# Other places for the block sums' steps around two norms, and the second layer's add copies in the pool of temporaries

## The chip, the cores and the metric

The kernel runs on one core of a Trainium2 chip. The metric is the device time of one execution in microseconds (us), less being better. The core has a matrix engine (TensorE, PE in the profile), a vector engine (VectorE, DVE), a scalar engine (ScalarE, ACT), GpSimd (POOL) and an engine that mostly issues loads (SyncE, SP). Each works off its own list of instructions in order and waits at semaphores for the others.

## The reference, cut to what matters

A two-layer encoder trunk on 512 tokens of width 1024. Each layer is a mixer (mLSTM and memory attention in layer 0; band attention and memory attention in layer 1), and then a gated feed-forward part with a causal convolution of width 3 over the tokens. The change touches the feed-forward part of both layers.

```python
D_MODEL, SEQ, DEPTH, D_FF, FFN_CONV = 1024, 512, 2, 2816, 3

def rmsnorm(x, g):
    y = x * lax.rsqrt(jnp.mean(x * x, axis=-1, keepdims=True) + 1e-6)
    return y * g

def conv_ffn(h, w_up, conv_w, conv_b, w_down):
    u, g = jnp.split(h @ w_up, 2, axis=-1)     # 1024 -> 2 x 2816
    g = causal_dwconv(g, conv_w, conv_b)       # 3 taps over the tokens
    return (jax.nn.silu(g) * u) @ w_down       # 2816 -> 1024
...
x = x + conv_ffn(rmsnorm(x, g_ffn), w_up, conv_w, conv_b, w_down)   # in each layer
...
return rmsnorm(x, final_g)
```

## The kernel before, in words

Activations are held with features on the 128 partitions and the 512 tokens along the free axis. Each fp32 number is split into a high and a low part of a shorter type, and a product is three matmuls (`mm3`: high by high at L197, high by low at L198, low by high at L199). The split is a cast on ScalarE (L143) and a subtract on VectorE (L144). Tiles of weights are loaded raw ("wr"), and split into "wh" and "wl". In the order's listings the number behind such a name counts the tiles, and what stands behind `<-` is read.

The feed-forward part has 22 tiles of 128 hidden features (`ChannelMixer`). The first three are "plain": `plain(j)` makes the gate and the up product with `project()`, 24 matmuls of 128x512 each, the gate in a bank of tag "mm" and the up in one of tag "sc". The other 19 go through `step()` in a fixed order (`manual_schedule`, which keeps the written order of PE, ACT and DVE). A step multiplies blocks as Strassen's method does: seven block products of 12 matmuls 128x256, the first into the bank `r1` with the weight block `a11`. They need sums of blocks of the activations, which `block_sums()` makes ahead of the first step, as a generator (`forms`) of four steps. Each step scales two tiles on ScalarE (L788), does four subtracts on VectorE (L797), and splits four halves (four L143, four L144).

Where these four steps stand is set in two places. `EARLY` says, for each layer, how many are taken while the mixer's output projection is finished, behind which of its eight tiles. The rest are woven into the plain tiles: `weave(job, filler, each)` takes one step of the filler each time `each` has added up to 1 over the yields of the job, and whatever is left runs behind the third tile. `plain(0)` also weaves in `norm.finish()`: a cast and a subtract of the sum of squares, two matmuls with a matrix of ones (L302), and a few ScalarE and VectorE instructions (from L304) that leave the row by which all hidden tiles are scaled. Outside of `manual_schedule` the order on each engine is set by a scheduler that places instructions by its own estimates, so what stands where is read from the listings below.

Down products belong to the steps too. `down_products` makes a partial sum of one of the eight output tiles in a PSUM bank "tr"; `add` copies the bank on ScalarE into an SBUF tile (L823), from which GpSimd issues a DMA that adds it to the residual in DRAM, `xspill` (L824). The first two steps of a layer have four such adds, later ones two, 40 in a layer. The tiles come from the tag "bias", which has four buffers. In layer 1 two of these hold the last norm's gains from before the feed-forward part to the end. In a step the bank `r1` is used five times in turn; L892 is ScalarE's copy that empties it after the first, and L883 that after later ones. Tiles of tag "t" are temporaries of 128x512, eight buffers: a step keeps `up`, `u3`, `pre` and an accumulator in them.

## Time and profile before

| | us |
|---|---|
| Median of 3 runs | 1186.98 |
| Lowest and highest run | 1186.8, 1188.5 |
| The profiled execution | 1186.16 |
| Its span in the profile | 1184.4 |
| TensorE busy in it | 1166.5 |
| Mean granted clock of TensorE | 0.998 |

The span runs from the first to the last instruction that the profile records. In the rows of a timeline stand the start, the duration, the engine, the line and the operation, the tiles written and read, the shape and, in brackets, how long the engine had stood idle before it and which instruction ended that. A matmul's row is longer than the distance to the next, since matmuls overlap. In the table of windows "PEclk" is the clock that TensorE was granted, as a share of full speed.

### The profile page before, as it was taken

How to read it: one execution, taken by the hardware profiler on the slowest of the kernel's cores; microseconds unless marked ns; L12 is line 12 of the kernel's file. 1: busy time of each engine (PE TensorE's matmuls, PEld its weight loads, DVE VectorE, ACT ScalarE, POOL GpSimd, SP SyncE). 2: the span in 40 equal slices, each digit the busy share in tenths (PEclk: the TensorE clock that was granted, in tenths of full speed). 3: DMA queues.
4: the chain of work that ended last, by engine and by line, in shares of the span. 5: the costliest groups of instructions: out<-in, count | busy, mean ns of one | idle time of the engine just before them, and what ended most of it. 6: DMA issues, size and time to landing. Idle time of an engine off the chain costs nothing.

```text
span 1184.4 us, 19103 instructions
## 1 busy us (share of the span) xinstructions
PE 1166.5 (98%) x7149; PEld 1037.1 (88%) x7149; DVE 984.5 (83%) x1768; ACT 744.1 (63%) x1345; POOL 143.3 (12%) x238
## 2 busy tenths in 40 slices
PE   9999999999999999999999999999989999999997
PEld 9988888887899999999888888778789999999986
DVE  6776788788999988888788888997888998888865
ACT  6448677656666655555666666775756665555545
POOL 1111101010032211111020000101011111111100
PEclk9999999999999999999999999999999999999999
DMA  8645325344478766655662323236345766666551
GB/s 290 216 110 147 77 54 151 85 144 118 109 176 198 187 166 166 143 142 117 177 209 86 89 72 107 79 118 188 115 109 108 174 145 143 143 142 143 125 160 72
DMA packets 200623, 162.87 MB, mean 138 GB/s; under 512 B 8680, under 2 KB 176334, under 8 KB 200530
## 3 DMA queue, kind: packets, MB, share of 16 engines
q1 hardware_dynamic: 182066, 119.74, 34.5%
q0 software_dynamic: 17888, 40.86, 18.0%
q8 instruction: 56, 0.92, 0.3%
q10 hardware_dynamic: 576, 1.05, 0.2%
q14 instruction: 37, 0.30, 0.1%
HBM read 128.89 MB, written 36.66 MB: 140 GB/s over the span
## 4 chain that ended last, share of the span: by engine, by line
PE 82%; issue 12%; DVE 2%; ACT 1%; POOL 1%; DMA 1%; POOLq 0%; ACTq 0%; DVEq 0%
PE pmm L197 16%; PE pmm L198 16%; PE pmm L199 16%; PE ptr L198 6%; PE ptr L197 5%; PE ptr L199 5%; PE psc L198 4%; PE psc L197 4%; PE psc L199 4%; PE psc L603 2%; PE ptr L1414 1%; DVE wl L144 1%; DMA xspill<-bias 1%; PE ptr L1435 0%; PE ptr L1436 0%
## 5 line engine op out<-in xcount | busy, mean ns | idle before, releaser
L197 PE MATMUL pmm<-u,wh 128*128 128x512 f32 (+1 forms) x984 | 334.4, 340 | 3.3 <-ACT wh L143 3.2
L199 PE MATMUL pmm<-u,wl 128*128 128x512 f32 (+1 forms) x984 | 331.9, 337 | 1.8 <-DVE wl L144 1.8
L198 PE MATMUL pmm<-u,wh 128*128 128x512 f32 (+1 forms) x984 | 331.4, 337 | 0.0
L144 DVE TENSOR_TENSOR wl<-wr,wh 128x1024 fp32r<-128x1024 f32 (+4 forms) x172 | 195.7, 1138 | 74.0 <-ACT wh L143 73.4
L143 ACT CAST wh<-wr 128x1024 fp32r<-128x1024 f32 (+4 forms) x172 | 168.3, 981 | 81.4 <-PE pmm L198 32.7
L199 PEld LDWEIGHTS pmm<-u,wl 128*128 128x128 f32 x984 | 184.8, 188 | 22.0 <-DVE wl L144 2.4
L197 PEld LDWEIGHTS pmm<-u,wh 128*128 128x128 f32 x984 | 184.9, 188 | 21.2 <-ACT wh L143 4.0
L198 PEld LDWEIGHTS pmm<-u,wh 128*128 128x128 f32 x984 | 185.0, 188 | 16.8 <-DVE u L144 0.5
L824 POOL DMA_DIRECT2D xspill<-bias x80 | 69.5, 886 | 424.3 <-ACT bias L823 398.4
L197 PE MATMUL ptr<-u,wh 128*128 128x512 f32 x272 | 106.6, 392 | 0.0
L198 PE MATMUL ptr<-u,wh 128*128 128x512 f32 x272 | 106.3, 391 | 0.0
L199 PE MATMUL ptr<-u,wl 128*128 128x512 f32 x272 | 105.8, 389 | 0.0
L143 ACT CAST fh<-pt 128x512 fp32r<-128x512 f32 x114 | 71.0, 625 | 32.7 <-DVE pt L942 32.3
L197 PE MATMUL pmm<-u,fh 128*128 128x256 f32 x304 | 85.0, 280 | 3.3 <-ACT t L892 3.3
L883 ACT COPY t<-pmm 128x256 f32<-128x256 f32 x114 | 42.7, 375 | 71.1 <-PE pmm L199 70.9
L144 DVE TENSOR_TENSOR fl<-pt,fh 128x512 fp32r<-128x512 f32 x114 | 78.3, 688 | 9.6 <-ACT fh L143 6.7
L198 PE MATMUL pmm<-u,fh 128*128 128x256 f32 x304 | 84.6, 278 | 0.0
L199 PE MATMUL pmm<-u,fl 128*128 128x256 f32 x304 | 84.5, 278 | 0.0
L744 DVE SCALAR_TENSOR_TENSOR t<-t,cols,t 128x511 f32<-128x511 f32 x88 | 65.9, 749 | 8.4 <-ACT t L751 7.1
L823 ACT COPY bias<-ptr 128x512 f32<-128x512 f32 x80 | 46.8, 588 | 40.2 <-PE ptr L199 34.7
L199 PE MATMUL psc<-u,wl 128*128 128x256 f32 (+1 forms) x216 | 67.3, 311 | 0.4 <-DVE wl L144 0.4
L197 PE MATMUL psc<-u,wh 128*128 128x256 f32 (+1 forms) x216 | 67.6, 313 | 0.0
(348 smaller groups left out, 2607.6 us busy)
## 6 DMA issues: line engine op xcount, KB each, us to landing
wr<-in_ffn_w_up_dram SPq DMA_DIRECT2D x50, 512.0 KB, 7.3
xspill<-bias POOLq DMA_DIRECT2D x80, 256.0 KB, 5.8
pt<-in_ffn_w_up_dram SPq DMA_DIRECT2D x38, 512.0 KB, 7.7
wr<-in_ffn_w_down_dram SPq DMA_DIRECT2D x34, 512.0 KB, 5.3
wr<-in_a_w_in_dram SPq DMA_DIRECT2D x20, 512.0 KB, 3.8
wr<-in_w_kv_dram SPq DMA_DIRECT2D x12, 512.0 KB, 4.0
xspill<-fh POOLq DMA_DIRECT2D x16, 256.0 KB, 2.6
xspill<-fl POOLq DMA_DIRECT2D x16, 256.0 KB, 2.6
```

Source lines behind the costliest of these rows:

```text
L143: high = A.copy(hi, src) if on_act else V.tensor_copy(hi, src)
L144: low = V.tensor_tensor(out=lo, in0=src, in1=f(hi), op=ALU.subtract)
L197: nc.tensor.matmul(o, lh, rh, start=first, stop=False, skip_group_check=more)
L198: nc.tensor.matmul(o, lh, rl, start=False, stop=False, skip_group_check=more)
L199: nc.tensor.matmul(o, ll, rh, start=False, stop=last, skip_group_check=more)
L603: nc.tensor.matmul(o, a, b, start=first and i == 0, stop=i == 1)
L744: V.scalar_tensor_tensor(acc[:, n:], src[:, : S - n], self.fw[:, c * FT + j : c * FT + j + 1], acc[:, n:], op0=ALU.mult, op1=ALU.add,)
L823: A.copy(t, o)
L824: G.dma_start(xspill[j], t, accum_op=ALU.add)
L883: A.copy(o, r[:, :H])
L1414: nc.tensor.transpose(tp[:, b * P : (b + 1) * P], es[T, h][:, b * P : (b + 1) * P], ident)
```

## The change

Four edits. `EARLY` takes one block-sum step fewer in each layer during the output projection (two are left in layer 0, one in layer 1). A new table `BEHIND_NORM` takes one step in each layer directly behind the weaving of `norm.finish()` in `plain(0)`. The rate of weaving goes from one step in 8 yields to one in 16. And `add` takes its tile in layer 1 from the tag "t" and no longer from "bias". The number of instructions is the same on every engine; lines from L766 on move down by two (L823 becomes L825, L892 becomes L894).

```diff
-EARLY = ({4: 1, 5: 1, 7: 1}, {7: 2})
+EARLY, BEHIND_NORM = ({4: 1, 5: 1}, {7: 1}), (1, 1)
...
             if self.norm.row is None:
                 both = pair_of(gate, up)
                 weave(self.norm.finish(), both, 1)
+                for _ in range(BEHIND_NORM[self.l]):
+                    next(self.forms)
                 og, ou = yield from both
...
         def add(self, j, o):
-            t = sb("bias", [P, S])
+            t = sb(("bias", "t")[self.l], [P, S])
             A.copy(t, o)
             G.dma_start(xspill[j], t, accum_op=ALU.add)
...
-        weave(mixer.plain(0), mixer.forms, 0.125)
+        weave(mixer.plain(0), mixer.forms, 0.0625)
...
-            weave(mixer.plain(j), mixer.forms, 0.125)
+            weave(mixer.plain(j), mixer.forms, 0.0625)
```

What this does to the order is shown at three places. The first is the norm in layer 1. TensorE's order behind the gate of tile 0 (`pmm1872` before, `pmm1864` after), before the change:

```order
L199 MATMUL pmm1872_9350<-u1847_9288,wl21871_9347 128x512
L197 MATMUL pmm1891_9440<-u1814_9132,wh21889_9436 128x512
L198 MATMUL pmm1891_9440<-u1815_9133,wh21889_9436 128x512
L197 MATMUL pmm1919_9559<-u1814_9132,wh11917_9555 128x512
L198 MATMUL pmm1919_9559<-u1815_9133,wh11917_9555 128x512
L199 MATMUL pmm1919_9559<-u1814_9132,wl11918_9556 128x512
L197 MATMUL pmm1919_9559<-u1817_9141,wh11917_9555 128x512
L199 MATMUL pmm1891_9440<-u1814_9132,wl21890_9437 128x512
L302 MATMUL psc1873_9372<-t1867_9340,onesr_90 128x512
L197 MATMUL psc1880_9391<-u1814_9132,wh01878_9387 128x512
```

And after:

```order
L199 MATMUL pmm1864_9328<-u1847_9288,wl21863_9325 128x512
L302 MATMUL psc1865_9350<-t1859_9318,onesr_90 128x512
L197 MATMUL psc1872_9369<-u1814_9132,wh01870_9365 128x512
L198 MATMUL psc1872_9369<-u1815_9133,wh01870_9365 128x512
L199 MATMUL psc1872_9369<-u1814_9132,wl01871_9366 128x512
L197 MATMUL psc1872_9369<-u1817_9141,wh01870_9365 128x512
L198 MATMUL psc1872_9369<-u1818_9142,wh01870_9365 128x512
L199 MATMUL psc1872_9369<-u1817_9141,wl01871_9366 128x512
L302 MATMUL psc1865_9350<-t1860_9319,onesr_90 128x512
```

Before, the gates of tile 1 (`pmm1891`) and tile 2 (`pmm1919`) began ahead of the ones-matmul (L302) and of the up product of tile 0 (`psc1880`); after, the ones-matmul and the up product (`psc1872`) come first. In layer 0 it is alike: before, matmuls of the gate of tile 1 stood ahead of the ones-matmuls and of the up product of tile 0; after, the ones-matmuls stand near the end of the gate of tile 0, and up 0, gate 1, up 1, gate 2 and up 2 follow one by one. ScalarE's order at the same place in layer 1, before:

```order
L143 CAST u1856_9311<-t1852_9297 128x256
L788 ACTIVATE u1857_9314<-fh1699_8668,cols0_449 128x512
L788 ACTIVATE u1858_9315<-fl1703_8676,cols0_449 128x512
L143 CAST wh21889_9436<-wr1888_9434 128x1024
L143 CAST u1861_9324<-t1859_9318 128x256
L143 CAST u1862_9327<-t1859_9318 128x256
L143 CAST u1863_9330<-t1860_9319 128x256
L143 CAST t1867_9340<-rb1813_9130 128x512
```

And after:

```order
L143 CAST u1856_9311<-t1852_9297 128x256
L143 CAST t1859_9318<-rb1813_9130 128x512
L790 ACTIVATE u1874_9382<-fh1699_8668,cols0_449 128x512
L790 ACTIVATE u1875_9383<-fl1703_8676,cols0_449 128x512
L143 CAST wh21889_9436<-wr1888_9434 128x1024
L304 ACTIVATE t1868_9355<-psc1865_9350,eps_97 128x512
```

The cast of the norm's sum of squares (from `rb1813`) has moved ahead of the second block sum's two scales and of the weights of tile 1's gate (`wh21889`). The second place is the end of the plain tiles in layer 1, on VectorE, where `wl01931` is the low half of the first step's up weights, `a11` among them. Before:

```order
L144 TENSOR_TENSOR u1911_9539<-t1908_9530,u1911_9539 128x256
L144 TENSOR_TENSOR u1912_9542<-t1909_9531,u1912_9542 128x256
L144 TENSOR_TENSOR u1913_9545<-t1909_9531,u1913_9545 128x256
L779 TENSOR_TENSOR t1900_9487<-psc1905_9501,t1900_9487 128x512
L744 SCALAR_TENSOR_TENSOR t1920_9584<-t1921_9585,cols2_805,t1920_9584 128x511
L144 TENSOR_TENSOR wl01931_9634<-wr1928_9629,wh01930_9633 128x1024
```

And after:

```order
L744 SCALAR_TENSOR_TENSOR t1892_9465<-t1893_9466,cols2_805,t1892_9465 128x510
L799 TENSOR_TENSOR t1900_9508<-u1898_9504 128x256
L144 TENSOR_TENSOR wl01931_9634<-wr1928_9629,wh01930_9633 128x1024
L778 TENSOR_TENSOR t1892_9465<-t1892_9465,rb1873_9380 128x512
L799 TENSOR_TENSOR t1900_9508<-u1899_9505,t1900_9508 128x256
```

Before, it came behind the last block sum's low halves (row 1345 of VectorE's order); now it stands at row 1326, behind the first subtract of the third sum. The third place is the adds of the first step of layer 1, on ScalarE, with the semaphores that each instruction waits for (DMASW are those of GpSimd's DMAs). Before:

```order
L823 COPY bias1958_9769<-ptr1954_9750 128x512 [waits DMASW2_49,PE_49]
L143 CAST fh1959_9772<-pt1886_9432 128x512
L823 COPY bias1961_9776<-ptr1955_9757 128x512 [waits DMASW3_49,PE_49]
L143 CAST wh21962_9779<-wr1941_9662 128x1024 [waits DMAHW6_49,PE_49,Activation_49]
L883 COPY t1949_9673<-pmm1944_9668 128x256
L823 COPY bias1966_9822<-ptr1964_9796 128x512 [waits DMASW6_49,Activation_49]
L823 COPY bias1967_9825<-ptr1965_9803 128x512 [waits DMASW7_49,PE_49,Activation_49]
L143 CAST fh1970_9835<-pt1887_9433 128x512 [waits DVE_49]
```

And after:

```order
L825 COPY t1958_9769<-ptr1954_9750 128x512 [waits PE_49]
L143 CAST fh1959_9772<-pt1886_9432 128x512
L825 COPY t1961_9776<-ptr1955_9757 128x512 [waits PE_49]
L143 CAST wh21962_9779<-wr1941_9662 128x1024 [waits DMAHW6_49,PE_49,Activation_49]
L885 COPY t1949_9673<-pmm1944_9668 128x256
L825 COPY t1966_9822<-ptr1964_9796 128x512 [waits Activation_49]
L825 COPY t1967_9825<-ptr1965_9803 128x512 [waits PE_49,Activation_49]
L143 CAST fh1970_9835<-pt1887_9433 128x512 [waits DVE_49]
```

The order is the same, and the copies wait for no DMA any more; they go into "t" buffers, which later instructions take.

## The prediction, on record before the run

> **What bounds the kernel now.** I read the page's head first, then the table of windows, then the timeline of TensorE at its gaps and of ScalarE ahead of each gap.

> ```profile
> span 1184.4 us, 19103 instructions
> ## 1 busy us (share of the span) xinstructions
> PE 1166.5 (98%) x7149; PEld 1037.1 (88%) x7149; DVE 984.5 (83%) x1768; ACT 744.1 (63%) x1345; POOL 143.3 (12%) x238
> ```

> TensorE is busy for 1166.5 of 1184.4 us, and the change takes no matmul away. So all that it can win is idle time of PE, 17.9 us in the whole span, and matmuls that ran at a lower clock. The question is how much of that lies in the stretches that the change touches: the plain tiles and the first steps behind them, in each layer. In the table below each row is a stretch: its length, each engine's busy time (instructions), the granted clock, the DMA share and GB/s.

> ```profile
> core 0: us, PE busy (x) PEld busy (x) DVE busy (x) ACT busy (x) POOL busy (x), PEclk, DMA share, GB/s
> 273.50:313.80 40.30, 38.36 (x184) 31.55 (x183) 34.47 (x57) 25.12 (x40) 1.66 (x3) 1.00 0.33 92
> 324.73:339.76 15.03, 15.03 (x110) 14.05 (x109) 13.22 (x20) 9.95 (x19) 4.73 (x6) 1.00 0.79 171
> 834.00:836.23 2.23, 0.00 (x1) 0.00 (x0) 2.23 (x7) 2.23 (x5) 0.00 (x0) 1.00 0.21 58
> 836.23:864.07 27.84, 27.84 (x123) 22.93 (x124) 24.28 (x47) 19.80 (x35) 0.00 (x0) 1.00 0.31 90
> 850.00:870.00 20.00, 18.76 (x102) 16.13 (x101) 18.37 (x34) 14.04 (x26) 0.00 (x0) 1.00 0.29 86
> 864.07:881.11 17.04, 15.80 (x109) 14.41 (x108) 14.53 (x21) 8.97 (x15) 1.74 (x2) 1.00 0.38 91
> 881.11:900.10 18.99, 16.94 (x111) 15.76 (x109) 13.40 (x20) 9.65 (x18) 3.41 (x4) 0.91 0.65 120
> 886.05:889.46 3.41, 3.41 (x17) 3.41 (x18) 3.34 (x6) 1.29 (x3) 0.30 (x1) 0.53 1.04 200
> 900.10:914.09 13.99, 12.76 (x99) 12.05 (x98) 11.05 (x18) 9.00 (x17) 3.21 (x4) 1.00 0.65 144
> 914.09:926.36 12.27, 12.27 (x99) 11.78 (x97) 12.12 (x21) 8.41 (x15) 1.73 (x3) 1.00 0.71 150
> 926.36:1157.00 230.64, 230.64 (x1647) 214.99 (x1646) 196.52 (x289) 132.82 (x225) 24.11 (x29) 1.00 0.62 145
> ```

> The windows from 864.07 on are bounded by the first `r1` matmul of a step. A step of 108 matmuls (84 of block products, 24 of down products) takes 15.03 us without a gap (the row at 324.73, layer 0), one of 96 takes 12.27 (914.09). The first two steps of layer 1 have 108 and take 17.04 and 18.99; the third has 96 and takes 13.99. Behind 914.09 PE does not idle up to 1157. So what there is to win lies in these places: 1.94 idle us in the plain tiles of layer 0, 2.23 in those of layer 1, and 2.01, 3.96 and 1.72 us above the undisturbed length in three steps of layer 1.

> **Layer 0, plain tiles.** PE's gaps, with what released each:

> ```profile
> 279.98 0.50 PE L197 MATMUL pmm<-u,wh 128*128 128x512 f32 x1 [0.95 <-ACT wh L143]
> ...
> 281.24 0.50 PE L199 MATMUL pmm<-u,wl 128*128 128x512 f32 x1 [0.53 <-DVE wl L144]
> ...
> 304.73 0.50 PE L199 MATMUL psc<-u,wl 128*128 128x512 f32 x1 [0.41 <-DVE wl L144]
> ```

> All three are waits for the halves of a weight tile, which ScalarE casts (L143) and VectorE subtracts (L144). Before, the scheduler took the gate of tile 1 ahead of the up tile of tile 0, so the weights of tile 1 were needed early, just where VectorE and ScalarE also made a block sum and the norm row. After, the two ones-matmuls of the norm stand in the end of gate 0, and up 0, gate 1, up 1, gate 2 and up 2 follow as unbroken tiles, so the weights of gate 1 have one tile more of time. One block sum fewer is made ahead of them (`EARLY` loses its 7:1), and the rest come at half the rate. I take all three gaps away: 1.9 us. Ends: 1.1 if the first is replaced by a wait of its middle size (0.53) and 0.3 of slow first matmuls; 2.2 if the first matmul behind each gap (0.50 long here) also comes back to normal. What is late next is DVE, with 34.47 of 40.30 us; no block sum has a matmul waiting for it ahead of the first step.

> **Layer 1, plain tiles.** ScalarE ahead of the largest gap, PE's gap, and the one behind the plain tiles:

> ```profile
> 833.91 0.72 ACT L788 ACTIVATE u<-fh,cols 128x512 f32<-128x512 f32 x1
> 834.53 0.71 ACT L788 ACTIVATE u<-fl,cols 128x512 f32<-128x512 f32 x1
> 835.15 1.03 ACT L143 CAST wh<-wr 128x1024 fp32r<-128x1024 f32 x1
> 836.08 1.08 ACT L143 CAST u<-t 128x256 fp32r<-128x256 f32 x3
> 837.06 0.62 ACT L143 CAST t<-rb 128x512 fp32r<-128x512 f32 x1
> ```

> ```profile
> 836.23 0.50 PE L197 MATMUL pmm<-u,wh 128*128 128x512 f32 x1 [2.23 <-ACT wh L143]
> ```

> ```profile
> 864.43 1.22 DVE L144 TENSOR_TENSOR wl<-wr,wh 128x1024 fp32r<-128x1024 f32 x1
> ```

> ```profile
> 865.70 0.39 PE L199 MATMUL pmm<-u,wl 128*128 128x256 f32 x1 [1.24 <-DVE wl L144]
> ```

> At 834.00 PE has nothing left but the gate of tile 1, whose weights ScalarE casts at 835.15, behind the two scales of a second early block sum (0.72 and 0.71, at L788). After, that sum is one of the steps behind the norm, and the cast of the norm's sum (0.62 at 837.06 before) takes the place of the scales at 833.91. It ends at 834.53, and the ones-matmul, which PE needs next, follows 0.05 later as at 836.23 (the cast's end 836.18). PE then waits 0.6 instead of 2.23 us: a gain of 1.6. The ends are 2.2 (no wait) and 0.9 (one scale of 0.72 still ahead). Up 0 comes next, whose weights were split before. The 1.24 at 865.70 is the low half of the first step's `a11`: VectorE made it last, at 864.43. After, its split stands 19 rows earlier in VectorE's order, within the third block sum (some 9 us by the rows' durations, an estimate), and only the last sum is left behind it. Of the 2.01 us above 15.03 in this step I take 1.5: the 1.24, and half of the 0.77 that no gap shows; ends 0 and 2.0.

> **Layer 1, the adds.** ScalarE in the first and second step (the line of the second fence is from the third), the waits of that stretch, and PE:

> ```profile
> 881.19 0.59 ACT L823 COPY bias<-ptr 128x512 f32<-128x512 f32 x1
> 884.62 0.59 ACT L823 COPY bias<-ptr 128x512 f32<-128x512 f32 x1 [2.84 <-DMA xspill<-bias]
> 885.10 0.62 ACT L143 CAST fh<-pt 128x512 fp32r<-128x512 f32 x1
> 885.62 0.38 ACT L892 COPY t<-pmm 128x256 f32<-128x256 f32 x1
> ```

> ```profile
> 902.78 0.59 ACT L823 COPY bias<-ptr 128x512 f32<-128x512 f32 x1 [2.37 <-DMA xspill<-bias]
> ```

> ```profile
> ACT bias L823 <- DMA xspill<-bias: 5.4, 3, 2.8
> ```

> ```profile
> 886.05 0.40 PE L197 MATMUL pmm<-u,fh 128*128 128x256 f32 x1 [2.05 <-ACT t L892]
> ...
> 904.21 0.39 PE L197 MATMUL pmm<-u,fh 128*128 128x256 f32 x1 [1.23 <-ACT t L892]
> ```

> Two of the four "bias" buffers hold the last norm's gains in this layer. The fourth copy of a step with four adds waits for the DMA of the second (2.84 us), and behind it on ScalarE stand a cast and the copy L892 that frees `r1`'s bank, for which PE waits 2.05. Once more 2.37 and 1.23 in the next step. After, the copies go into four of the eight "t" buffers, and the order shows no DMA among the waits of the first four. Both waits go. The second step also ran its 3.41 us behind the gap at a granted clock of 0.53, which costs about 3.41 × 0.47 = 1.6; with 2.05 that is 3.65 of its 3.96 us. If the dip comes from the gap, it goes too. I take 3.9 for this step and 1.7 of 1.72 for the next; ends 2.0 and 4.0, and 1.2 and 1.7.

> [...]

> What the new place costs: a "t" buffer comes free only when its DMA has landed, and now the copies of the steps' sums (L885, L894 after) can wait for that.

> ```profile
> wr<-in_ffn_w_up_dram SPq DMA_DIRECT2D x50, 512.0 KB, 7.3
> xspill<-bias POOLq DMA_DIRECT2D x80, 256.0 KB, 5.8
> pt<-in_ffn_w_up_dram SPq DMA_DIRECT2D x38, 512.0 KB, 7.7
> ```

> From issue to landing an add takes 5.8 us in the middle. In the order the buffer of an add is next used by the `u3` or `pre` copy of the following step, or by the next step's add: 12 us or more behind the issue, a step being 12.27 or 15.03 long. That leaves 6 us to spare, so I cost it at 0; if DMAs took twice as long the cover would be gone. POOL issues the same 40 adds, up to 3 us earlier in the first steps. On SP one up load moves ahead of one gate load (7.3 and 7.7 us to landing, in a stretch with a DMA share near 0.3): 0, at most the 0.4 between them.

> **Sum.** 1.9 + 1.6 + 1.5 + 3.9 + 1.7 = 10.6 us. The profiled execution took 1186.16 (span 1184.4 and 1.8 around it), so after 1175.6; the median of the runs is 0.8 above the profiled one, so 1176.4 for a median.

> **The rivals.** First, VectorE is the bound where the sums now go: it was busy 18.37 of 20 us from 850 to 870, and the last block sum now falls near the end of that. If the low half of `a11`, or the last sum's low halves, come as late as before, the 1.5 is not won, and a late sum adds its four subtracts and the four low halves, up to 0.4 each: about 1.5 + 1.3 given back, 1179.2. Against it: one sum fewer stands ahead of the norm, and the change takes no work on DVE into these stretches that was not there, only another order of it.
> Second, the dip of the clock is no child of the gap and stays, or moves to the 0.6 us gap: 1.6 lost, 1178.0. For it speaks that a longer gap had none; against it, that it begins with the first matmul behind the gap.
> Third, the plain tiles win nothing, since one wait for a weight is replaced by another, and only the adds work: 5.6 gained, 1181.4.
> Fourth, on the other side: the "t" pool, now with up to eight live buffers, has the `u3` copy wait for an add's DMA in every step of layer 1, with PE behind it as at 886.05. At 2.05 us a step, 19 steps cost 39 us and the time would be near 1215; it decides from the sixth step on that pays it (10.6 / 2.05 = 5.2). Against it are the 12 us between issue and reuse. [...]
> Fifth, nothing changes since PE's waits only move on: 1187.

> **How the numbers follow.** Forecast 0.56, DVE 0.16 (1179.2), clock 0.10 (1178.0), adds alone 0.09 (1181.4), the pool 0.05, nothing 0.04. The forecast's own range is 1174.9 to 1177.9: all the upper ends together are 2.2 + 2.2 + 2.0 + 4.0 + 1.7 = 12.1 us, and 0.8 less in layer 0 with 0.7 less at the norm are 9.1. Of the range the lower end lies 1.1 below that, about as far as the runs shown differ from their middle (1186.8 to 1188.5), and the upper end leaves out half of the adds-alone case, all of the pool and the last: 1173.8 to 1181.0. A difference of 0.2% is 2.4 us, about what a measurement of this kernel tells from no change. Faster: the first four, 0.91. Within: the last, 0.04. Slower: the pool, 0.05.

> **What would show it.** Right: in the profile after, PE has no gap in the plain tiles of layer 0 and one of about 0.6 ahead of the ones-matmul (L302) of layer 1; the steps of layer 1 take 15.0 to 15.6, 15.1 and 12.3; the waits list no DMA ahead of the add's copy (L825 now) there, and the clock shows no 0.53. PE's busy time falls by the dip's 1.6, its idle time to near 9 us. Wrong: a wait for L144 at the first step's `a11` or third product (DVE), a dip elsewhere (clock), new waits for a weight's cast in the plain tiles (adds alone), or waits of L885 for an add's DMA in step after step (the pool).

## The result, and the profile after

The changed kernel takes 1174.97 us in the median (1174.31 to 1175.42, four runs), the kernel before 1186.89 (1185.85 to 1188.5, four runs). The ratio is 0.9898 with an interval of 0.9881 to 0.9915, some 12 us less. The forecast was 1176.4 in a range of 1173.8 to 1181.0. The profiled execution took 1175.14.

The head of the page after, and the stretches in the table of windows. The first row is a window as long as the one before, and as far ahead of layer 0's second step (10.93 us); the next five are bounded by the gap and by the first `r1` matmuls of the steps, as before; the last runs from the fourth step on:

```profile
span 1173.4 us, 19109 instructions
## 1 busy us (share of the span) xinstructions
PE 1163.2 (99%) x7149; PEld 1035.1 (88%) x7149; DVE 983.8 (84%) x1768; ACT 744.2 (63%) x1345; POOL 143.0 (12%) x238
```

```profile
core 0: us, PE busy (x) PEld busy (x) DVE busy (x) ACT busy (x) POOL busy (x), PEclk, DMA share, GB/s
270.92:311.22 40.30, 40.30 (x198) 34.07 (x197) 36.72 (x64) 27.09 (x45) 1.65 (x3) 1.00 0.40 114
831.40:832.15 0.75, 0.00 (x0) 0.00 (x0) 0.75 (x2) 0.75 (x3) 0.00 (x0) 1.00 0.00 0
832.15:859.93 27.78, 27.77 (x122) 23.02 (x123) 26.81 (x49) 21.16 (x34) 0.00 (x0) 1.00 0.38 114
859.93:875.73 15.80, 15.78 (x110) 14.39 (x108) 13.28 (x24) 9.55 (x19) 1.73 (x2) 1.00 0.27 54
875.73:890.76 15.03, 15.03 (x111) 14.05 (x110) 13.22 (x20) 9.88 (x19) 3.44 (x4) 1.00 0.81 162
890.76:903.03 12.27, 12.27 (x99) 11.78 (x97) 11.34 (x18) 8.74 (x17) 3.29 (x4) 1.00 0.76 166
903.03:1146.00 242.97, 242.97 (x1743) 226.83 (x1742) 208.52 (x308) 141.35 (x240) 25.73 (x31) 1.00 0.63 146
```

In the plain tiles of layer 0 PE is now busy for all of the 40.30 us (38.36 before), and runs 198 matmuls in them (184). In layer 1 the wait of 2.23 us has become one of 0.75, and the first three steps take 15.80, 15.03 and 12.27 us where they took 17.04, 18.99 and 13.99. None of these stretches shows a clock under 1.00. PE's busy time fell by 3.3 us (1166.5 to 1163.2) and its idle time to 10.2; the prediction's signs were 1.6 and near 9, and its 15.0 to 15.6 for the first step was missed too. Of the seven gaps before, one is left in the stretches of the change; ScalarE's rows and PE's show what ends it:

```profile
830.57 1.01 ACT L143 CAST u<-t 128x256 fp32r<-128x256 f32 x3
831.49 0.61 ACT L143 CAST t<-rb 128x512 fp32r<-128x512 f32 x1
832.01 0.72 ACT L790 ACTIVATE u<-fh,cols 128x512 f32<-128x512 f32 x1
```

```profile
832.15 0.50 PE L302 MATMUL psc<-t,onesr 128*128 128x512 f32 x1 [0.76 <-ACT t L143]
```

The cast of the norm's sum stands ahead of the second sum's scales, as the order said, and still behind the casts of the first. The waits of ScalarE for the adds' DMAs in layer 1, 5.4 us in three waits before, are gone. The view of all that waited for the adds after names nobody; landing took

```profile
DMA to landing us min/median/max: 3.3/5.4/8.8
```

so the eight "t" buffers cover even the slowest add.

### The profile page after: what moved, and what is told of

The parts are those of the page before. It is cut to its first block, busy times and chain, and to the rows that moved or that the text cites. A ratio compares the mean times of both kernels' runs of the same rounds, so it can differ in the third digit from the quotient of the medians.

```text
span 1173.4 us, 19109 instructions
## 1 busy us (share of the span) xinstructions
PE 1163.2 (99%) x7149; PEld 1035.1 (88%) x7149; DVE 983.8 (84%) x1768; ACT 744.2 (63%) x1345; POOL 143.0 (12%) x238
## 3 DMA queue, kind: packets, MB, share of 16 engines
q10 hardware_dynamic: 576, 1.05, 0.2%
## 4 chain that ended last, share of the span: by engine, by line
PE 96%; DVE 2%; ACT 1%; DMA 0%; issue 0%; POOL 0%; POOLq 0%; DVEq 0%
PE pmm L197 19%; PE pmm L198 18%; PE pmm L199 18%; PE ptr L198 6%; PE ptr L197 6%; PE ptr L199 6%; PE psc L198 5%; PE psc L199 5%; PE psc L197 5%; PE psc L603 2%; PE ptr L1416 1%; PE ptr L1437 1%; PE ptr L1438 1%; PE ptr L672 1%; PE pmm L494 0%; PE ptr L686 0%
## 5 line engine op out<-in xcount | busy, mean ns | idle before, releaser
L197 PE MATMUL pmm<-u,wh 128*128 128x512 f32 (+1 forms) x984 | 334.2, 340 | 0.2 <-ACT u L143 0.2
L199 PE MATMUL pmm<-u,wl 128*128 128x512 f32 (+1 forms) x984 | 331.6, 337 | 0.0
L144 DVE TENSOR_TENSOR wl<-wr,wh 128x1024 fp32r<-128x1024 f32 (+4 forms) x172 | 195.8, 1138 | 74.9 <-ACT wh L143 74.2
L143 ACT CAST wh<-wr 128x1024 fp32r<-128x1024 f32 (+4 forms) x172 | 168.5, 982 | 78.8 <-PE pmm L198 30.8
L199 PEld LDWEIGHTS pmm<-u,wl 128*128 128x128 f32 x984 | 184.8, 188 | 19.5
L197 PEld LDWEIGHTS pmm<-u,wh 128*128 128x128 f32 x984 | 184.9, 188 | 17.3 <-ACT u L143 1.0
L197 PE MATMUL ptr<-u,wh 128*128 128x512 f32 x272 | 106.6, 392 | 0.0
L199 PE MATMUL ptr<-u,wl 128*128 128x512 f32 x272 | 105.8, 389 | 0.0
L143 ACT CAST fh<-pt 128x512 fp32r<-128x512 f32 x114 | 71.3, 626 | 34.4 <-DVE pt L944 33.6
L885 ACT COPY t<-pmm 128x256 f32<-128x256 f32 x114 | 42.5, 373 | 69.4 <-PE pmm L199 69.1
L197 PE MATMUL pmm<-u,fh 128*128 128x256 f32 x304 | 84.4, 278 | 0.0
L199 PE MATMUL pmm<-u,fl 128*128 128x256 f32 x304 | 84.0, 276 | 0.0
L144 DVE TENSOR_TENSOR fl<-pt,fh 128x512 fp32r<-128x512 f32 x114 | 78.4, 688 | 4.3 <-ACT fh L143 1.4
L197 PE MATMUL psc<-u,wh 128*128 128x256 f32 (+1 forms) x216 | 67.2, 311 | 0.0
L198 PE MATMUL psc<-u,wh 128*128 128x256 f32 (+1 forms) x216 | 67.0, 310 | 0.0
L199 PE MATMUL psc<-u,wl 128*128 128x256 f32 (+1 forms) x216 | 67.0, 310 | 0.0
L826 POOL DMA_DIRECT2D xspill<-t x40 | 34.2, 870 | 258.0 <-ACT t L825 244.8
## 6 DMA issues: line engine op xcount, KB each, us to landing
wr<-in_ffn_w_up_dram SPq DMA_DIRECT2D x50, 512.0 KB, 8.2
pt<-in_ffn_w_up_dram SPq DMA_DIRECT2D x38, 512.0 KB, 8.1
wr<-in_ffn_w_down_dram SPq DMA_DIRECT2D x34, 512.0 KB, 5.5
wr<-in_a_w_in_dram SPq DMA_DIRECT2D x20, 512.0 KB, 3.9
xspill<-bias POOLq DMA_DIRECT2D x40, 256.0 KB, 6.1
xspill<-t POOLq DMA_DIRECT2D x40, 256.0 KB, 5.9
wr<-in_w_kv_dram SPq DMA_DIRECT2D x12, 512.0 KB, 4.0
xspill<-fh POOLq DMA_DIRECT2D x16, 256.0 KB, 2.6
```

Source lines behind the costliest of these rows:

```text
L143: high = A.copy(hi, src) if on_act else V.tensor_copy(hi, src)
L144: low = V.tensor_tensor(out=lo, in0=src, in1=f(hi), op=ALU.subtract)
L197: nc.tensor.matmul(o, lh, rh, start=first, stop=False, skip_group_check=more)
L198: nc.tensor.matmul(o, lh, rl, start=False, stop=False, skip_group_check=more)
L199: nc.tensor.matmul(o, ll, rh, start=False, stop=last, skip_group_check=more)
L826: G.dma_start(xspill[j], t, accum_op=ALU.add)
```

## The experiments

All but the two that add gaps were timed against runs of the kernel before on the same chip. A difference in us is worked out from the ratio, not from the medians; the two are up to 0.6 us apart. First the parts of the change alone. **The adds alone**:

```diff
-            t = sb("bias", [P, S])
+            t = sb(("bias", "t")[self.l], [P, S])
```

> The kernel before with one edit: add takes its tile from t in layer 1; the block sums stand as before. Theory A (the five terms are separate waits and add up): the two steps of layer 1 with waits behind the add's copy go from 18.99 and 13.99 us to 15.03 and 12.27, the granted clock of 0.53 behind the 2.05 us gap goes too, and the gaps of the plain tiles stay (0.95, 0.53, 0.41, 2.23, 1.24): 3.96 + 1.72 = 5.7 us less than before, ratio 0.9952. Rival B (the t pool is short, and the plain order only hid it): waits of L883 for an add's DMA show, and the gain is under 3 us. Rival C (the dip of the clock is not a child of the gap): it stays somewhere in these steps and the gain is 4.1 us.

Measured: 1181.55 us against 1186.41, ratio 0.9954 (0.9941 to 0.9968), 5.5 us less. The two steps take what theory A says, and the first, whose late `a11` was not touched, is as before:

```profile
866.70:883.73 17.03, 15.80 (x109) 14.51 (x108) 14.51 (x21) 8.99 (x16) 1.73 (x2) 1.00 0.36 87
883.73:898.76 15.03, 15.03 (x111) 14.05 (x109) 13.22 (x20) 9.88 (x19) 3.44 (x4) 1.00 0.81 152
898.76:911.03 12.27, 12.27 (x98) 11.78 (x97) 11.34 (x18) 8.75 (x17) 3.29 (x4) 1.00 0.81 171
```

No copy waits for a DMA, so rival B falls. But a half clock (0.50) was seen in this profile too, behind the other large gap, that of the plain tiles: it was 2.86 us long here, and in the profile of before, at 2.23, no half clock had followed it.

**The block sums alone** (`add` back to "bias"):

> The changed kernel with one edit undone: add keeps bias in layer 1. Theory A: the plain tiles stand as in the changed kernel, the adds wait as before: the r1 steps of layer 1 take about 15.8, 18.99 and 13.99 us; 2.6 + 1.5 + 1.2 = 5.3 us less than before, ratio 0.9955; the 2 us gap is there again, and with it the dip to about half the clock for 3.4 us. Rival C: the gap is there and the clock stays at 1.00, since the dip belonged to something else; then 1.6 us more are won, 6.9 less than before.

Measured: 1179.38, ratio 0.9937 (0.9924 to 0.995), 7.5 us less, more than theory A's 5.3. PE's waits behind the adds are there, the first shorter (2.05 before) and the second longer (1.23), and the clock stayed at 1.00:

```profile
880.57 0.38 PE L197 MATMUL pmm<-u,fh 128*128 128x256 f32 x1 [1.62 <-ACT t L894]
...
897.64 0.39 PE L197 MATMUL pmm<-u,fh 128*128 128x256 f32 x1 [1.77 <-ACT t L894]
```

So it looked like rival C, that the dip belongs to something else; the gap experiments below decide against that.

**Layer 0 alone** (`EARLY`, `BEHIND_NORM` and the rate changed for layer 0 only, "bias" kept):

> Only the block sums of layer 0 are placed as in the changed kernel (one early step fewer, one behind the norm, a step in 16 yields); layer 1 and the adds are as before. Theory A: the three gaps of layer 0 go, and each gave back its idle time and some 0.2 us of restart: 2.5 us less than before, ratio 0.998. Rival D (the layers are not separate: what layer 0 gains, a transfer or the mixer of layer 1 takes back): under 1 us.

Measured: 1183.14, ratio 0.997 (0.996 to 0.998), 3.6 us less with an interval of 2.4 to 4.7, so rival D falls; theory A's 2.5 lies near the lower end. The three gaps of layer 0 are gone, those of layer 1 stay. The profiled execution had two windows of 3.41 us at half clock (0.50), behind gaps of 2.22 and 1.94 us.

**The rate alone** (`mixer.forms, 0.125` to `0.0625`, all else as before):

> The kernel before with one edit: one block-sum step in 16 yields and no longer in 8; the early steps, bias and all else as before. In the order the gate of tile 1 still stands ahead of the up product of tile 0 in both layers, and the low half of the first step's a11 in layer 1 moves ahead of the last sums. Theory A: the gaps of 0.95 and 2.23 stay, those of 0.41 (layer 0) and 1.24 (layer 1) go, each with some 0.2 us of restart, and the adds wait as before: 1.5 to 2.1 us less, ratio 0.998 to 0.9985. Rival G (the rate alone frees the plain tiles): 4 us and more.

Measured: 1184.13, ratio 0.998 (0.9969 to 0.9991), 2.4 us less. The gaps of 0.41 and 1.24 went and those of 0.95 and 2.31 stayed, as theory A said. PE's waits behind the adds were not quite as before (0.86 and 1.61 for 2.05 and 1.23). The profiled execution is the fastest of the twelve (1181.98). **All but the rate** (the changed kernel with 0.125):

> The changed kernel with the rate of weaving put back to one step in 8 yields; the step behind the norm, the early steps and the adds in t as changed. The order of the plain tiles stays the changed one. Theory A: what matters is the step behind the norm, and the rate is worth under 1 us beside it: 1174.5 to 1176. Rival G: the gap at the first step's a11 (1.24) is there again, 1176.5.

Measured: 1175.85, ratio 0.9911 (0.9894 to 0.9928). No gap at `a11`; rival G falls in both. The step behind the norm, with one early step fewer, carries the plain tiles; the rate is worth about 1 us beside it, which lies within the intervals.

Next, whether the adds' gain is a matter of the number of free buffers. **The last norm's gains loaded later**, the adds in "bias":

```diff
-    fgb = [sb("bias", [P, S]) for _ in range(2)]
-    for hf in range(2):
-        G.dma_start(fgb[hf], bass.AP(tensor=final_g.tensor, offset=final_g.offset + hf * S, ap=[[0, P], [1, S]]))
...
     hid = channel_mixer(mixer)
+    fgb = [sb("bias", [P, S]) for _ in range(2)]
+    for hf in range(2):
+        G.dma_start(fgb[hf], bass.AP(tensor=final_g.tensor, offset=final_g.offset + hf * S, ap=[[0, P], [1, S]]))
```

> The kernel before with one edit: the last norm's gains are loaded behind the feed-forward part of layer 1, so that all four bias buffers are free in its steps; the adds stay in bias. Theory A (the waits are a matter of how many buffers an add can take, not of which pool): no wait of the add's copy for a DMA, steps of 15.03 and 12.27 us, and the time of the kernel with the adds in t alone, 1181.5, ratio about 0.995. Rival B (the t pool also changes something else, for instance when the steps' copies run): the waits go, and the time is over 1 us from that kernel's.

Measured: 1182.55, ratio 0.996 (0.9946 to 0.9973). No wait of an add for a DMA, and the steps take 15.03 and 12.27. Against the adds in "t" alone (0.9954) the intervals overlap. The medians are 1.0 us apart, just at the sign of rival B, so to within 1 us the number of free buffers is what counts. **Two "t" buffers fewer** in the steps of layer 1, where `later()` now takes them for the gains ahead of the first step:

```diff
+            for hf in range(2 * self.l):
+                fgb[hf] = sb("t", [P, S])
+                load_gain(hf)
             prep, tail = Forms(self, PLAIN), None
```

> The changed kernel with two of the eight t buffers taken out of use in the steps of layer 1 (the last norm's gains are loaded into them at the start of the steps). Theory A (an add's DMA lands some 5 us after its issue and the buffer is next taken 12 us or more later in most steps): in the first two steps the copy L897 into up now takes the buffer of an add issued 5 us before, and waits 0 to 1.5 us; in later steps nothing: 0 to 2 us more than the changed kernel, 1175 to 1177. Rival B (the pool was just large enough): PE waits in every step, 10 us and more on top.

Measured: 1177.14, ratio 0.9917 (0.9904 to 0.9929): about 2 us over the changed kernel, just past the end of theory A's band (1177). The size was nearly right and the place wrong. What waits is not the copy L897 but the accumulator, L751, twice:

```profile
ACT t L751 <- DMA xspill<-t: 3.4, 2, 2.4
```

The second step takes 15.12 us and the third 14.10, with one gap of PE of 1.26. In later steps no copy waits for an add's DMA. The pool has room for two buffers less, but for the first steps' eight adds.

Then the late sums. **No early sum in layer 1** (`EARLY` `({4: 1, 5: 1}, {})`):

> The changed kernel with no block sum of layer 1 during the output projection (its EARLY entry is empty): one stands behind the norm, two in the plain tiles, the last behind them. It takes the two scales, four casts and the subtracts away from ahead of the norm's cast. Theory A: the 0.76 us gap at the ones-matmul goes (1.0 with its restart), and VectorE, busy 26.81 of 27.78 us in the plain tiles, cannot take another sum of some 2.8 us: the last low halves come late for the third product of the first step, a gap of 1 to 2.5 us there, so 0 to 1.5 us slower than the changed kernel. Rival F (VectorE has room): 1 us faster.

Measured: 1180.25, ratio 0.9944 (0.9932 to 0.9956): 5 us over the changed kernel, more than either theory. The 0.76 went, and this came:

```profile
863.92 0.39 PE L197 MATMUL pmm<-u,fh 128*128 128x256 f32 x1 [2.62 <-ACT t L894]
...
866.73 0.58 PE L198 MATMUL pmm<-u,fh 128*128 128x256 f32 x1 [0.59 <-DVE u L144]
```

ScalarE's copy L894 of the first step now stands behind the last sum's two scales, and these behind a cast that waited 1.05 us for VectorE (L781). This is the prediction's first rival, VectorE as the bound, reaching PE by way of ScalarE; behind the gap came two windows of 3.41 us at half clock (0.50), some 3 us of loss (an estimate: half of each, but for 0.59 of idle time in the first). **The early sum two tiles sooner**, `{5: 1}`, and **three tiles sooner**, `{4: 1}`, as tries to win the last 0.76:

> The changed kernel with the one early sum of layer 1 two tiles of the output projection earlier (EARLY of layer 1 is 5:1 and no longer 7:1). In the order, ScalarE's cast of the norm's sum then stands behind one scale and no longer behind a sum's casts and a weight's cast, and the first ones-matmul stands ahead of the last three matmuls of gate 0. Theory A: the 0.76 us gap ahead of the ones-matmul goes, with 0.2 of restart, and nothing else moves: 0.8 to 1.0 us faster than the changed kernel, about 1174.0. Rival H (the sum is in the way where it now stands, with scales and casts ahead of what gate 0 waits for): a gap in gate 0 of 0.5 us or more, no gain.

> The changed kernel with the one early sum of layer 1 three tiles of the output projection earlier (4:1). Theory A: as with 5:1, the 0.76 us gap goes, 0.8 to 1.0 us faster than the changed kernel. Rival H: VectorE and ScalarE are late for the scaled activations of gate 0, a gap there, no gain or a loss of 0.5 to 1 us.

Measured: 1179.97, ratio 0.9942 (0.9926 to 0.9957), and 1182.04, ratio 0.9961 (0.9946 to 0.9977). Both lose 5 to 7 us to the changed kernel. The gap at the ones-matmul is gone in both, and each has one new gap, with two windows at half clock (0.50) behind it:

```profile
865.78 0.58 PE L197 MATMUL pmm<-u,fh 128*128 128x256 f32 x1 [3.89 <-ACT t L894]
```

```profile
826.02 0.79 PE L199 MATMUL pmm<-u,wl 128*128 128x512 f32 x1 [4.62 <-DVE wl L144]
```

With 5:1 my expectation missed: the scheduler's estimates, moved by one sum, put a weight's cast that waits 1.72 us for VectorE (L944) ahead of the first step's L894, where the changed kernel has it behind. With 4:1 the wait is neither where rival H put it nor for what it named, the scaled activations of gate 0. It is for a weight's low half, in the output projection's last tile ahead of gate 0: VectorE starts this half at 824.74, behind the block sum, and the tile's add (L716) follows at 834.05. None of these beats the changed kernel.

Last, the clock. **Added gaps**, two kernels that are instruments:

```diff
+            for _ in range(EXTRA.get(j, 0)):
+                A.copy(new.up, self.norm.row)
             A.copy(new.up[:, :H], r1[:, :H])
```

> An instrument, not a version: the changed kernel with 2 to 9 extra copies of a 128x512 tile on ScalarE ahead of the copy that empties r1 in the steps 6 to 21 of each layer (the real copy then overwrites their target). PE idles in each such step for about the copies' time less 1.1 us that the second product covers: from 0 to about 3.4 us, 32 gaps in one run, at various moments. Theory A (a gap of PE is followed by the half clock by chance of where it falls against a fixed window of about 3.4 us): gaps under about 1.5 us are never followed by it, gaps of 2 to 3 us sometimes, those over 3 us nearly always, each dip 3.4 us long. Rival C (the dip has nothing to do with gaps): no dips behind them, or at places without a gap. [...]

> The instrument again, with copies chosen so that nearly all added gaps of PE are between 1.8 and 2.6 us, some 25 of them. Theory A, as the runs so far put it (the clock is judged over fixed windows of 3.413 us that run on through the whole execution, and is halved for one window if PE was idle in the one before for more than some 1.87 us): a gap is followed by a dip just where 1.87 us or more of it lie in one such window, the windows being read off from the dips' own edges; near 6 in 10 of the gaps of 2.45 us, none of those of 1.8. Rival E (the length of the gap decides, with scatter): dips fall without regard to the windows.

In the first, four of the gaps were followed by a half clock: those of 3.10 and 3.45 us; none of 2.45 or less was. In the second, gaps of one length behaved differently: of 22 gaps of 2.45 us, 10 were followed by a half clock and 12 were not. In each run with several dips their ends lie on one grid of 3.413 us; in the second kernel the residual is at most 0.01 us over 18 dips in 887 us. Two gaps of 2.45 us in the second kernel, each with the grid's window that holds most of it and the window behind:

```profile
553.23:556.64 3.41, 1.61 (x13) 1.61 (x14) 0.88 (x2) 2.37 (x5) 0.00 (x0) 1.00 0.87 221
556.64:560.05 3.41, 3.41 (x28) 3.32 (x28) 3.29 (x6) 2.06 (x5) 0.00 (x0) 1.00 0.02 5
1109.61:1113.02 3.41, 1.57 (x13) 1.57 (x14) 0.84 (x2) 2.41 (x5) 0.00 (x0) 1.00 0.83 218
1113.02:1116.43 3.41, 3.41 (x19) 3.41 (x18) 3.29 (x6) 1.62 (x3) 0.00 (x0) 0.50 0.00 0
```

PE busy 1.61 us of a window (idle 1.80): the next runs at full clock, 28 matmuls. PE busy 1.57 (idle 1.85): the next at 0.50, 19 matmuls. Over the nine profiles with a dip there are 66 gaps of 0.8 us or more. The 36 that left no window with more than 1.80 us of idle time had no dip behind them; the 30 that left one with 1.85 or more all had one. In one of these the window's idle time, 1.91 us, is the sum of two gaps. So in these 66 it was the idle time in one window, length and phase together, that told the gaps with a dip from those without: theory A, with 1.80 to 1.85 us where it had some 1.87. Rivals C and E fall.

## Why the prediction was right

**The dip of the clock.** The prediction took it as a child of the gap, with the undisturbed 2.23 us gap against it. The grid settles both in the same profile of before. The 2.05 us gap lay whole in one window, with PE busy for 1.36; the 2.23 us gap fell across an edge, 1.09 and 1.14:

```profile
831.68:835.09 3.41, 2.32 (x11) 1.58 (x9) 3.27 (x9) 3.41 (x8) 0.00 (x0) 1.00 0.00 0
835.09:838.50 3.41, 2.27 (x10) 1.81 (x11) 3.41 (x9) 3.00 (x7) 0.00 (x0) 1.00 0.52 154
882.88:886.29 3.41, 1.36 (x12) 1.16 (x12) 0.66 (x2) 1.67 (x4) 0.84 (x2) 1.00 1.09 294
886.29:889.70 3.41, 3.41 (x18) 3.41 (x18) 3.34 (x7) 1.29 (x3) 0.06 (x1) 0.50 0.96 181
```

What the step got wrong is that it is no fixed price. The gap of the plain tiles had no dip behind it before (2.23 us) and one with layer 0 alone changed (2.22), where the gap of the adds (1.94) had one too; each dip is worth half of 3.41, 1.7 us. So that the 1.6 came out in full is luck in part: the profiled execution happened to hold one dip. The scatter agrees: 42 executions of the kernel before, timed beside the experiments, ran from 1184.19 to 1189.24 us, the ten under 1185 at a mean clock of 0.999, the ten over 1188 at 0.995 to 0.997, while the changed kernel's four runs lie within 1.1 us. No trace of these executions is on record, so that dips make this scatter is argued, not shown. The mean clock is a rough sign at that: the changed kernel's profile, without a dip ahead of PE's last matmul, has 0.998, and shows 0.50 from 1170.00 to 1173.40, where no matmul runs. The block sums alone fit in: their gaps of 1.62 and 1.77 us are under the 1.80 of idle time that had no dip behind it.

**Layer 0.** Forecast 1.9, ends 1.1 and 2.2. The same two matmuls, one ahead of the plain tiles and the first of the second step, before and then after:

```profile
255.51 0.39 PE L199 MATMUL ptr<-u,wl 128*128 128x512 f32 x1
...
324.73 0.28 PE L197 MATMUL pmm<-u,wh 128*128 128x256 f32 x1
```

```profile
255.86 0.39 PE L199 MATMUL ptr<-u,wl 128*128 128x512 f32 x1
...
322.15 0.28 PE L197 MATMUL pmm<-u,wh 128*128 128x256 f32 x1
```

They are 69.22 us apart before and 66.29 after: 2.9 us, over the term's upper end (the execution after was 0.34 late at the first of them, which it had been since its first 30 us). With layer 0 alone changed the distance is 66.21. All three gaps went, as said; the term was mis-sized, since each of these gaps cost more than its idle time. PE's next matmul would have begun some 0.16 us before the end of the last (rows of 0.39 us stand 0.23 apart), and the first behind each of these gaps took longer (0.50 for 0.39): 0.27 us for each of three gaps, 0.8 beside the 1.9 of idle time. The prediction had only the slower matmul, and that only in the upper end.

**Layer 1, plain tiles.** From the end of gate 0 to the first step it was 30.07 us (834.00 to 864.07) and is 28.53 (831.40 to 859.93): 1.54, forecast 1.6. The wait left is 0.76, forecast 0.6. In the first step 1.24 was won, forecast 1.5 (a sum that was off by itself: 1.24 and half of 0.77 are 1.6). The late `a11` went with its restart, 1.5 in all, but PE's weight loads now wait at two places in this step, so shortly that the overlap hides the gap:

```profile
862.80 0.19 PEld L197 LDWEIGHTS pmm<-u,fh 128*128 128x128 f32 x1 [0.18 <-ACT t L894]
...
871.51 0.19 PEld L197 LDWEIGHTS ptr<-u,wh 128*128 128x128 f32 x1 [0.22 <-ACT t L825]
```

The second was there before; the first is new, and the start of its matmul and of the next are 0.25 us late in all.

**The adds.** 18.99 to 15.03 and 13.99 to 12.27 are 3.96 and 1.72, forecast 3.9 and 1.7, and the first of the two holds the dip that this execution happened to have.

**The sum.** 2.9 + 1.5 + 1.2 + 4.0 + 1.7 = 11.3, less the 0.3 by which the execution after was late ahead of the plain tiles: 11.0, the difference of the spans (1184.4 less 1173.4), against 10.6. The median moved 11.9. The prediction carried over the 0.8 by which the profiled execution was under the median; after, it lies 0.2 over it. That the other runs of before held more dips would explain it, and is not shown. PE's busy time fell by 3.3 us where 1.6 was forecast: the restarts of the six gaps that went, 0.27 each, count as busy too.

**The rivals.** The pool: nothing waits for an add after, and with six buffers only the first steps pay. VectorE: it is as full as feared (26.81 of 27.78 us), and the version without an early sum shows the price; the last low halves were in time in the changed kernel. The adds alone: 5.5, forecast 5.6 for that case.

## What to carry to other kernels

On an engine that is busy for 98% the gain of a reordering can be read gap by gap, from what released each and what stands ahead of it on the releaser's engine; each gap's restart comes on top (0.27 us here). Where copies wait for DMAs that read their buffers, count free buffers and the time from issue to reuse, and take them from whichever pool has them. A new order that removes one small gap may move an unrelated copy behind a late cast, as the tries for 0.76 us did at a price of 5 to 7 us, half clocks included: look at what stands ahead of the first copy that PE needs in every stage behind the edit.
